# TensorE's MLP matmuls in program-text order instead of the scheduler's order

## The chip, the cores and the metric

The kernel runs on one core of a Trainium2 chip. The metric is the device time of one launch in microseconds (us): 2710.55 us, the median of three runs (2709.97 to 2710.85). Lower is better.

## The reference

One layer of a streaming encoder over 2048 prompt rows and 32 sample rows (2080 rows, width 1024). Phase 1 of the kernel computes the first five lines; the change concerns the sixth and seventh:

```
h  = RMSNorm(x);  p = h @ w_in                      # one combined projection
a  = pooling(p)      b = banded attention(p)
c  = gated DeltaNet(p)   d = GLA(p)
x  = x + concat(a, b, c, d) @ w_out
x2 = x
x  = x2 + square(relu(RMSNorm(x2) @ w_up)) @ w_down # hidden width 4096
y  = RMSNorm(x)
```

## The kernel before, in words

**Precision.** Each fp32 operand of a matmul is split in two: ScalarE (ACT) copies it to a rounded `hi` (L252), VectorE (DVE) subtracts to get `lo` (L253). A product is three matmuls: hi·hi, hi·lo, lo·hi.

**Tiling of the MLP** (`phase2`). Three blocks of rows: 696, 696 and 688 wide, each in two halves of h = 348, 348 or 344 columns. A block takes 16 steps f2 of 256 hidden units each:

- `mlp_up` (L1756) forms a step's hidden units with seven products of half-size operands instead of eight (a Strassen-Winograd scheme): (A11, B11), (A12, B21), (s2, T2), (s1, T1), (s3, T3), (s4, B22), (A22, T4). Each product is 12 matmuls of 128 x h, so a step has 84. They accumulate in three PSUM tiles (`ps` 1, 2 and 4 of a pool with one buffer each). ACT saves partial totals (L1779), DVE adds a saved one and a PSUM tile (L1782, `total`), squares (L1786) and splits the hidden units into the tile `u`.
- `mlp_down` (L1807) of the step before multiplies its two `u` tiles by w_down: 16 groups (two halves of 8) of 6 matmuls, 96 in all. Each group has its own PSUM tile `d` from a pool of **three** buffers (`pdn`); a DVE add (L1821) evicts it into the accumulators `acc`. In the last step of block 2 the two last downs are one, with 12 matmuls a group.
- The weights of a step are loaded by SP, `up_begin` (L1693) forms sums of w_up's quarters on GpSimd (POOL, L1699), and `up_weights` (L1706) splits them: five splits of 128x1024 and one of 128x512 a step on DVE.

**Beside the steps.** From f2 = 3 of blocks 0 and 1 on, for some four steps, the generator `mlp_keep` (L1644) normalises the next block's rows: squares on ACT (L1592), adds on DVE (L1594), sums (L1626 to L1638), stores to DRAM. In f2 = 15, `mlp_prep` (L1659) loads these back and splits them into `h2T` (14 pieces). After the last down of a block, `final` (L1842) normalises each half: `rstd` (L1566) sums squares over the partitions with three fp32 ones-matmuls (`g<-fs,c`), ACT takes Ln and Exp (L1572, L1573), and eight DVE multiplies (L1850) scale the rows, which are stored.

**What sets the order.** The program is written as a text of instructions; a scheduler reorders each engine's instructions by its own estimates and inserts the semaphores. Each engine then works strictly in its own order. In the text, the loop writes all of `mlp_up(f2)`, then all of `mlp_down` of f2 - 1, and the helper jobs' instructions where `tick` and `next(side)` call them. The scheduler's order for TensorE (PE) mixes up and down matmuls.

Of the kernel before, what the change touches and what calls it, by code (L numbers as in the profile page):

```python
# [110 lines left out]
class K:  # L111
# [1559 lines left out]
    def phase2(self):  # L1671
        nc, tc, a = self.nc, self.tc, self.a
        with ExitStack() as ctx:
# [168 lines left out]
            def final(acc, ts, t0, fs, end):  # L1842
                self.rstd(fs, ts.stop - ts.start)
                for i in range(8):
# [6 lines left out]
                    self.store(a["o_y"][i][:, t0 + ts.start:t0 + ts.stop], x, 2, eng=nc.scalar if end and i % 2 else nc.sync)  # L1851
                    yield 1

            for blk in range(3):
                _, n, h, _ = self.span(blk)
                chs = [slice(0, h), slice(h, n)]
                side = None
                us = []
                for f2 in range(17 if blk < 2 else 16):
                    if f2 == 15 and blk < 2:  # L1860
                        for _ in side:
                            pass
                        while not self.ready(("cb", blk + 1)):
                            self.tick()
                        side = self.mlp_prep(blk + 1, hT)
                    nxt = mlp_up(f2, h, side if f2 == 15 else None) if f2 < 16 else []
                    if blk < 2 and f2 == 3:
                        side = self.mlp_keep(blk + 1)
                    if f2 == 1 and blk:
                        self.drain(True)  # L1870
                        acc = []
                        for _ in self.mlp_acc(blk, acc):
                            pass
                    if f2 == 15 and blk == 2:

                        mlp_down(us + nxt, acc, chs, blk)
                    elif us:
                        mlp_down(us, acc, chs, blk, side)
                    us = nxt
                for _ in side or ():  # L1880
                    pass
# [80 lines left out]
```

## Time and profile before

| | |
|---|---|
| median time | 2710.55 us |
| profiled execution | 2718.81 us, of which the span is 2717.0 us |
| PE / DVE / ACT / POOL busy, share of the span | 96% / 72% / 40% / 32% |
| PE matmuls in the whole program | 17012 |
| chain that ended last | PE 48%, DVE 6%, DMA 4% |
| mean granted PE clock | 0.977 |

The profiled execution is 8.26 us above the median, all rows below are from it. "Busy" of PE counts matmuls; the weight loads (PEld) run beside them. In a timeline row the two first numbers are start and length in us, `x2` says that two instructions are joined in the row, and the bracket is the idle time of that engine before it and what ended it. The MLP runs from about 1277 us to the end.

### The profile page before, as it was taken

To read this page: it belongs to the slowest core of one execution; us is meant where nothing else is said; L and a number is where in the kernel's file an instruction comes from. 1 tells how busy PE (TensorE), PEld (TensorE's weight loads), DVE (VectorE), ACT (ScalarE), POOL (GpSimd) and SP (SyncE) were. 2 spreads that over 40 slices of the span, in tenths; PEclk is the share of its full clock that TensorE was granted. 3 is DMA by queue.
4 is the path that set the end of the run, shared out by engine and by line. 5 is a ranking of instruction groups with operands and counts; after the bars stand their busy time and mean duration, and the time that the engine had idled before them with its cause. 6 is when DMAs were issued, how large, how long until landed. Compare 5 with 4: busy or idle time off the path is not lost.

```text
span 2717.0 us, 44750 instructions
## 1 busy us (share of the span) xinstructions
PE 2598.6 (96%) x17012; PEld 2420.9 (89%) x17012; DVE 1958.6 (72%) x3498; ACT 1077.2 (40%) x1934; POOL 871.0 (32%) x1064
## 2 busy tenths in 40 slices
PE   7999998999899999998999999999999999999998
PEld 7887787788788877878999999988999999999998
DVE  6567778878886865566787667778767777766675
ACT  6435643653465343343433223442233343323232
POOL 4533564464446443322121112222212213221111
PEclk9998998999999989999999999999999999999999
DMA  5555454454545566366353222455222235222221
GB/s 166 172 152 161 125 177 147 130 156 139 152 136 164 156 174 197 110 203 210 105 179 114 70 70 80 137 173 174 94 70 86 73 109 162 78 63 86 71 72 48
DMA packets 229144, 349.21 MB, mean 129 GB/s; under 512 B 52032, under 2 KB 152784, under 8 KB 228928
## 3 DMA queue, kind: packets, MB, share of 16 engines
q1 hardware_dynamic: 162384, 295.49, 36.2%
q10 hardware_dynamic: 66480, 50.78, 5.7%
q8 instruction: 134, 2.20, 0.3%
q14 instruction: 82, 0.67, 0.1%
q0 software_dynamic: 64, 0.08, 0.0%
HBM read 273.83 MB, written 73.56 MB: 128 GB/s over the span
## 4 chain that ended last, share of the span: by engine, by line
PE 48%; DVE 6%; DMA 4%; issue 2%; ACT 1%; POOL 1%; SPq 0%; DVEq 0%; ACTq 0%; POOLq 0%
PE d L90 24%; PE u L90 19%; PE g L90 3%; DVE wx L253 1%; DVE acc L1821 1%; DVE wt L253 1%; DMA ldt<-w_o 1%; DVE h2T L253 1%; DMA x2d<-sg 1%; DVE acc L1850 1%; PE l L90 0%; DMA cb<-cbd 0%; POOL wur L1699 0%; DMA acc<-x2d 0%; DMA wur<-w_up 0%
## 5 line engine op out<-in xcount | busy, mean ns | idle before, releaser
L90 PE MATMUL d<-u,wt 128*128 128x348 f32 (+1 forms) x2400 | 631.1, 323 | 6.5 <-DVE acc L1821 5.6
L90 PE MATMUL d<-u,wx 128*128 128x348 f32 (+1 forms) x2208 | 601.8, 324 | 6.2 <-DVE acc L1821 6.1
L90 PE MATMUL g<-hT,wt 128*128 128x512 f32 (+2 forms) x2544 | 545.8, 363 | 16.4 <-DVE sg L1421 6.5
L1821 DVE TENSOR_TENSOR acc<-acc,d 128x348 f32<-128x348 f32 (+1 forms) x752 | 375.3, 510 | 210.5 <-PE d L90 203.0
L90 PE MATMUL u<-h2T,wt 128*128 128x348 f32 (+1 forms) x2024 | 515.0, 323 | 9.9 <-DVE wt L253 7.4
L90 PE MATMUL u<-h2T,wx 128*128 128x348 f32 (+1 forms) x2008 | 513.1, 323 | 1.3 <-ACT wt L252 0.8
L90 PEld LDWEIGHTS g<-hT,wt 128*128 128x128 f32 x2544 | 415.8, 195 | 79.5 <-DVE hT L256 5.6
L90 PEld LDWEIGHTS d<-u,wt 128*128 128x128 f32 x2400 | 428.0, 189 | 9.8 <-DVE acc L1821 7.4
L90 PEld LDWEIGHTS d<-u,wx 128*128 128x128 f32 x2208 | 397.3, 189 | 9.8 <-DVE acc L1821 9.2
L90 PEld LDWEIGHTS u<-h2T,wt 128*128 128x128 f32 x2024 | 357.3, 189 | 11.9 <-DVE wt L253 8.3
L90 PEld LDWEIGHTS u<-h2T,wx 128*128 128x128 f32 x2008 | 355.7, 189 | 2.7 <-ACT wt L252 1.0
L1699 POOL TENSOR_TENSOR s<-wur 128x512 f32<-128x512 f32 x48 | 72.4, 1508 | 642.3 <-DMA wur<-w_up 511.0
L90 PE MATMUL g<-wt,hT 128*128 128x256 f32 (+3 forms) x1632 | 246.6, 300 | 6.2 <-DVE sg L464 3.2
L90 PEld LDWEIGHTS g<-wt,hT 128*128 128x128 f32 (+1 forms) x1632 | 216.5, 191 | 16.1 <-DVE sg L464 3.9
L253 DVE TENSOR_TENSOR wt<-ldt,wt 128x1024 fp32r<-128x1024 f32 (+1 forms) x120 | 162.7, 1356 | 74.3 <-ACT wt L252 72.2
L252 ACT CAST wt<-wur 128x1024 fp32r<-128x1024 f32 x126 | 131.4, 1049 | 204.7 <-PE u L90 156.7
L1699 POOL TENSOR_TENSOR wur<-s,wur 128x512 f32<-128x512 f32 x48 | 65.3, 1361 | 418.6 <-DVE wt L253 220.4
L252 ACT CAST wx<-wur 128x1024 fp32r<-128x1024 f32 x114 | 118.8, 1048 | 202.8 <-PE u L90 164.2
L253 DVE TENSOR_TENSOR wx<-wur,wt 128x1024 fp32r<-128x1024 f32 x125 | 160.8, 1286 | 29.9 <-PE u L90 10.7
L252 ACT CAST wt<-ldt 128x1024 fp32r<-128x1024 f32 (+1 forms) x120 | 125.9, 1049 | 121.3 <-PE g L90 83.9
L253 DVE TENSOR_TENSOR wt<-wur,wx 128x1024 fp32r<-128x1024 f32 x114 | 146.5, 1288 | 31.9 <-PE u L90 14.7
L1779 ACT COPY k<-u 128x348 f32<-128x348 f32 (+1 forms) x144 | 64.1, 447 | 265.1 <-PE u L90 264.1
(348 smaller groups left out, 3819.8 us busy)
## 6 DMA issues: line engine op xcount, KB each, us to landing
wur<-w_up SPq DMA_DIRECT2D x96, 512.0 KB, 3.7
wur<-w_down SPq DMA_DIRECT2D x96, 512.0 KB, 3.7
ldt<-w_fm SPq DMA_DIRECT2D x56, 512.0 KB, 4.4
ldt<-w_o SPq DMA_DIRECT2D x32, 512.0 KB, 4.8
ldt<-w_tm SPq DMA_DIRECT2D x24, 512.0 KB, 4.0
fmd<-sg ACTq DMA_DIRECT2D x46, 256.0 KB, 2.9
qkr<-fmd SPq DMA_DIRECT2D x88, 128.0 KB, 3.6
tmd<-sg ACTq DMA_DIRECT2D x64, 128.0 KB, 2.8
```

Of the source, the lines that this page charges most:

```text
L90: return self.order(self.k.nc.tensor.matmul(out, lhsT, rhs, start=not have, stop=True, skip_group_check=True))
L252: nc.scalar.copy(hi, src)
L253: (eng or nc.vector).tensor_tensor(lo, src, hi.bitcast(F32), ALU.subtract)
L1699: add = lambda o, x, y: nc.gpsimd.tensor_tensor(o, x, y, ALU.add)
L1779: nc.scalar.copy(keep[n], ps[z].t[:, :h])
L1821: nc.vector.tensor_tensor(x, x, ps.t[:, :cw], ALU.add)
L1850: nc.vector.scalar_tensor_tensor(x, x, self.fg[:, i:i + 1], fs[0], ALU.mult, ALU.mult)
```

## The change

One line: before the loop over blocks, TensorE's instructions are put under a manual schedule, in which they stand in the order of the text. The other engines' orders still come from the scheduler, which now plans around PE's fixed order. No instruction is added or removed, on any engine.

```diff
+            ctx.enter_context(tc.manual_schedule(engines={mybir.EngineType.PE}))
             for blk in range(3):
                 _, n, h, _ = self.span(blk)
```

PE's order before, in the steady part of block 0: in step 8's up, `u_727`, `u_726`, `u_728` are its PSUM tiles, and `d_...` are groups of the down.

```order
L90 MATMUL u_726_15903<-h2T,wx 128x348
L90 MATMUL d_15762<-u,wx 128x348 x2
L90 MATMUL d_15762<-u,wt 128x348
L90 MATMUL d_15762<-u,wx 128x348 x2
L90 MATMUL d_15762<-u,wt 128x348
L90 MATMUL u_726_15903<-h2T,wx 128x348
L90 MATMUL u_726_15903<-h2T,wt 128x348
L90 MATMUL d_15770<-u,wx 128x348 x2
L90 MATMUL d_15770<-u,wt 128x348
L90 MATMUL d_15770<-u,wx 128x348 x2
L90 MATMUL d_15770<-u,wt 128x348
```

The same step's PE order now, at the end of its up and the first two groups of the down behind it (tile numbers differ by two):

```order
L90 MATMUL u_726_15905<-h2T,wt 128x348 x2
L90 MATMUL u_726_15905<-h2T,wx 128x348
L90 MATMUL d_16022<-u,wt 128x348 x2
L90 MATMUL d_16022<-u,wx 128x348
L90 MATMUL d_16022<-u,wt 128x348 x2
L90 MATMUL d_16022<-u,wx 128x348
L90 MATMUL d_16030<-u,wt 128x348 x2
L90 MATMUL d_16030<-u,wx 128x348
L90 MATMUL d_16030<-u,wt 128x348 x2
L90 MATMUL d_16030<-u,wx 128x348
```

Before, groups of a down stood between pieces of the next up; now 84 up matmuls are followed by 16 groups in one run.

DVE's order before, around the totals of the same up (`c<-k,u_...` is L1782, `acc<-acc,d_...` evicts a group):

```order
L1782 TENSOR_TENSOR c<-k,u_726_15903 128x348
L1821 TENSOR_TENSOR acc<-acc,d_15812 128x348
L1782 TENSOR_TENSOR c<-k,u_728_15905 128x348
L1786 SCALAR_TENSOR_TENSOR c<-c 128x696
L1821 TENSOR_TENSOR acc<-acc,d_15825 128x348
L253 TENSOR_TENSOR wx<-wur,wt 128x1024
L1821 TENSOR_TENSOR acc<-acc,d_15833 128x348
L1821 TENSOR_TENSOR acc<-acc,d_15842 128x348
L1786 SCALAR_TENSOR_TENSOR c<-c 128x696
L1821 TENSOR_TENSOR acc<-acc,d_15850 128x348
```

And now:

```order
L1782 TENSOR_TENSOR c<-k,u_728_15907 128x348
L1786 SCALAR_TENSOR_TENSOR c<-c 128x696
L253 TENSOR_TENSOR wt<-s_16170,wt 128x512
L253 TENSOR_TENSOR wt<-wur,wx 128x1024
L253 TENSOR_TENSOR u<-c,u 128x696
L1821 TENSOR_TENSOR acc<-acc,d_16022 128x348
L1786 SCALAR_TENSOR_TENSOR c<-c 128x696
L1821 TENSOR_TENSOR acc<-acc,d_16030 128x348
L1821 TENSOR_TENSOR acc<-acc,d_16039 128x348
L1821 TENSOR_TENSOR acc<-acc,d_16047 128x348
L253 TENSOR_TENSOR u<-c,u 128x696
```

The evictions, which were spread over the step, now stand in its second part; a square, two weight splits and a split of `u` stand ahead of the first of them.

DVE's order before at the end of block 0: `d_18480` is the eighth group of the last down, whose squares feed `rstd` of the first half.

```order
L1821 TENSOR_TENSOR acc<-acc,d_18480 128x348
L1836 TENSOR_TENSOR fs<-fs,sq 128x348
L1821 TENSOR_TENSOR acc<-acc,d_18497 128x348
L1821 TENSOR_TENSOR acc<-acc,d_18508 128x348
L1821 TENSOR_TENSOR acc<-acc,d_18520 128x348
L253 TENSOR_TENSOR wx<-wur,wt 128x1024
L1821 TENSOR_TENSOR acc<-acc,d_18533 128x348
L1821 TENSOR_TENSOR acc<-acc,d_18546 128x348
L1850 SCALAR_TENSOR_TENSOR acc<-acc,pv,fs 128x348 x8
L1821 TENSOR_TENSOR acc<-acc,d_18559 128x348
```

And now (`d_18482` is the eighth group):

```order
L1821 TENSOR_TENSOR acc<-acc,d_18482 128x348
L1836 TENSOR_TENSOR fs<-fs,sq 128x348
L1850 SCALAR_TENSOR_TENSOR acc<-acc,pv,fs 128x348 x8
L1821 TENSOR_TENSOR acc<-acc,d_18499 128x348
L1821 TENSOR_TENSOR acc<-acc,d_18510 128x348
L1821 TENSOR_TENSOR acc<-acc,d_18522 128x348
L1821 TENSOR_TENSOR acc<-acc,d_18535 128x348
```

The eight multiplies of `final` moved from behind the fifth eviction of the second half to ahead of the first. On PE the three matmuls of `rstd` moved with them: before, they stood behind the group `d_18533`, the fourth of the second half; now they stand directly behind `d_18482`:

```order
L90 MATMUL d_18482<-u,wt 128x348 x2
L90 MATMUL d_18482<-u,wx 128x348
L90 MATMUL g_18492<-fs,c 128x348 x2
L90 MATMUL g_18492<-sq,c 128x348
L90 MATMUL d_18499<-u,wt 128x348 x2
L90 MATMUL d_18499<-u,wx 128x348
```

Phase 1 and the out projection keep their order, but for two up matmuls ahead of the last out projection tile.

## Rows read from the trace of the kernel before

**Rows 1.** Busy time by stretch: us, busy by engine, granted PE clock, DMA.

```profile
1277.00:1440.00 163.00, 159.45 (x987) 156.02 (x986) 129.11 (x181) 62.40 (x89) 41.69 (x27) 1.00 0.48 150
1440.00:1700.00 260.00, 260.00 (x1636) 260.00 (x1634) 180.25 (x271) 79.92 (x111) 51.77 (x36) 1.00 0.26 77
1700.00:1910.00 210.00, 196.03 (x1162) 191.22 (x1162) 168.93 (x241) 78.99 (x120) 52.25 (x36) 0.97 0.51 158
1910.00:2190.00 280.00, 280.00 (x1757) 280.00 (x1756) 199.19 (x293) 91.55 (x126) 55.46 (x36) 1.00 0.29 88
2190.00:2300.00 110.00, 103.66 (x614) 100.99 (x613) 86.06 (x123) 43.19 (x67) 34.42 (x24) 0.95 0.42 130
2300.00:2670.00 370.00, 370.00 (x2350) 369.69 (x2349) 245.84 (x380) 109.84 (x152) 66.47 (x48) 1.00 0.23 70
2670.00:2717.00 47.00, 36.25 (x217) 34.00 (x215) 22.57 (x40) 13.74 (x26) 7.60 (x8) 0.92 0.17 61
```

**Rows 2.** PE's waits in the MLP: total us, times, longest.

```profile
PE d L90 <- DVE acc L1821: 11.6, 10, 2.5
PE u L90 <- DVE wt L253: 7.4, 3, 4.0
```

**Rows 3.** Chain of waits, steady part: start, length, what.

```profile
1503.01 2.87 PE d L90 x18
```

**Rows 4.** DVE's timeline in a steady step.

```profile
1569.66 0.88 DVE L1786 SCALAR_TENSOR_TENSOR c<-c 128x696 f32<-128x696 f32 x1
1570.47 1.22 DVE L253 TENSOR_TENSOR wt<-wur,wx 128x1024 fp32r<-128x1024 f32 x1
1571.60 0.51 DVE L1821 TENSOR_TENSOR acc<-acc,d 128x348 f32<-128x348 f32 x1
1572.51 0.52 DVE L1821 TENSOR_TENSOR acc<-acc,d 128x348 f32<-128x348 f32 x1 [0.40 <-PE d L90]
1572.95 0.92 DVE L253 TENSOR_TENSOR u<-c,u 128x696 fp32r<-128x696 f32 x1
1573.79 1.97 DVE L1786 SCALAR_TENSOR_TENSOR c<-c 128x696 f32<-128x696 f32 x1
...
1578.96 0.68 DVE L253 TENSOR_TENSOR wx<-s,wx 128x512 fp32r<-128x512 f32 x1
```

**Rows 5.** POOL's timeline in the same step.

```profile
1573.20 1.81 POOL L1699 TENSOR_TENSOR wur<-wur 128x512 f32<-128x512 f32 x1
```

**Rows 6.** DVE groups of the side jobs: count, busy us, mean ns, idle before.

```profile
L253 DVE TENSOR_TENSOR h2T<-cb,h2T 128x688 fp32r<-128x688 f32 x14 | 13.1, 945 | 2.3 <-ACT h2T L252 2.3
...
L1594 DVE TENSOR_TENSOR nss<-nss,xp 128x688 f32<-128x688 f32 x7 | 6.1, 871 | 4.6 <-ACT xp L1592 4.6
```

**Rows 7.** PE's timeline after a long and after a short wait.

```profile
1720.06 0.95 PE L90 MATMUL d<-u,wt 128*128 128x348 f32 x2 [2.25 <-DVE acc L1821]
...
1731.62 0.43 PE L90 MATMUL u<-h2T,wx 128*128 128x348 f32 x1 [0.50 <-DVE wx L253]
1731.89 0.48 PE L90 MATMUL u<-h2T,wt 128*128 128x348 f32 x2
```

**Rows 8.** PE's timeline: rstd in block 0, and at the kernel's end.

```profile
1768.43 1.33 PE L90 MATMUL g<-fs,c 128*128 128x348 f32 x4
...
2703.92 0.33 PE L90 MATMUL d<-u,wx 128*128 128x344 f32 x1
2705.74 1.42 PE L90 MATMUL g<-fs,c 128*128 128x344 f32 x4 [1.50 <-POOL fs L1836]
2707.00 0.74 PE L90 MATMUL g<-sq,c 128*128 128x344 f32 x2
```

**Rows 9.** DVE's timeline: the multiplies of final.

```profile
1772.37 5.78 DVE L1850 SCALAR_TENSOR_TENSOR acc<-acc,pv,fs 128x348 f32<-128x348 f32 x8 [0.52 <-ACT fs L1573]
...
2693.83 3.99 DVE L1850 SCALAR_TENSOR_TENSOR acc<-acc,pv,fs 128x344 f32<-128x344 f32 x8 [0.43 <-ACT fs L1573]
...
2708.88 4.42 DVE L1850 SCALAR_TENSOR_TENSOR acc<-acc,pv,fs 128x344 f32<-128x344 f32 x6 [4.09 <-ACT fs L1573]
```

## The prediction, made before the changed kernel ran

> **What bounds the kernel now.** I read the page's shares first: PE is busy 96% of the span, so the question is where the other 4% lies. The busy time by stretch answers that [rows 1]: from 1440 to 1700, 1910 to 2190 and 2300 to 2670 us PE is busy for all of 910 us. There is nothing to gain in them. PE's idle time in the MLP lies in four places: 163.00 - 159.45 = 3.6 us where the MLP begins, 210.00 - 196.03 = 14.0 around the end of block 0, 110.00 - 103.66 = 6.3 around the end of block 1, and 47.00 - 36.25 = 10.8 at the end. The last is nearly all the final norm after the last down matmul at 2703.92 [rows 8], which both orders have. So 23.9 us of idle time could go.
>
> Beside it lie slow matmuls. The granted clock's column gives 0.97 around the end of block 0 and 0.95 around that of block 1 [rows 1], so 0.03 x 210 + 0.05 x 110 = 11.8 us at most (part of it falls on idle time). PE's timeline shows what they are: after a wait of 2.25 us two matmuls take 0.95 us, after one of 0.50 us two take 0.48 [rows 7]. The first pair is at the lower level of 1.2 GHz, the second at 2.4 GHz. All that the old order loses ahead of the final norm is therefore 23.9 + 11.8 = 35.7 us. PE's list of waits says what it waits for: ten times an eviction (11.6 us) and three times a weight split (7.4 us) [rows 2], both DVE's work.
>
> At full speed 18 matmuls take 2.87 us in the chain of waits [rows 3], so one takes 0.1595. A product of 12 takes 1.91 us, an up of 84 13.4, a group of 6 0.96 and a down of 96 15.3; a step is 28.7 us.
>
> **The change part by part.** No instruction goes or comes. PE's 84 up matmuls are now one run, and its 16 groups another. This asks something new of DVE: the evictions all come within 15.3 us, one each 0.96 us, and three PSUM buffers let PE run three groups, 2.87 us, ahead. DVE has the capacity: in the clean stretches it is busy 180.25 of 260, 199.19 of 280 and 245.84 of 370 us [rows 1], 66 to 71%. The issue is what stands ahead of the evictions in its strict order.
>
> *Regular steps.* DVE instructions that follow each other without a wait start about 0.08 us before the end of the one ahead (1569.66 + 0.88 against 1570.47 [rows 4]); so a square costs 0.81, a 128x1024 split 1.13, the 128x512 split 0.60, a split of `u` 0.84 and an eviction or a total 0.43. An eviction starts about 0.36 us after its group's last matmul starts, which is also what I take for a total. The up's sixth product is done after 6 x 1.91 = 11.5 us, its total starts at 11.7. By the order now shown: square to 13.1, 128x512 split to 13.8, 128x1024 split to 14.95, split of `u` to 15.75, first eviction 15.66 to 16.2. PE has begun group 0 at 13.4 and wants a fourth buffer at 13.4 + 2.87 = 16.27: it waits some 0.06 us. The second square runs to 17.0, the second eviction to 17.4; PE wants its buffer at 17.23 and waits about 0.27. After that DVE needs 0.43 an eviction against PE's 0.96 and catches up. That is 0.33 us a step; 31 steps have this order of DVE: **10 us**.
>
> The bounds: nothing, if the square and the splits are a little earlier, and 1 us a step (31 us) if they are stretched. The stretch is in the trace: a square takes 0.88 us alone and 1.97 beside POOL's sum at 1573.20 [rows 4, 5]. POOL's next sums should start, by the time the raw weights land, about 19 us into the step, behind the two dangerous evictions; hence the low value.
>
> The Trainium skill ("SBUF — State Buffer", "Who interferes with whom") says that a DVE instruction with two inputs in SBUF excludes a GpSimd instruction that reads SBUF, for the whole instruction, and that one with a single SBUF input does not. The squares and splits are of the first kind and the 1.97 us agrees; an eviction, with one input in PSUM, is not, so by this rule only what stands ahead of evictions is stretched. It is the first rival below.
>
> *Weights.* In text order the splits for the next up have a whole down, 15.3 us, as lead, and `acc` loads of the next block a whole up more. The waits for weights [rows 2] and those around the block changes go. What remains is the start, where the first steps come as fast as before: **2 us** of the 3.6.
>
> *Side jobs in the first half of blocks 0 and 1.* `mlp_keep`'s adds on DVE wait for rows from DRAM through ACT, 4.6 us for seven in the old order [rows 6]. There, up matmuls were at hand for PE whenever an eviction was late; now an add that waits in DVE's queue holds the evictions behind it, and PE stops 2.87 us later. Reading the new DVE order with these durations I get 2.5, 0.5, 1.5 and 2.6 us for its four downs, so 7 a block: **14 us**, between 0 (rows early) and 20.
>
> *h2T.* In f2 = 15, DVE has 14 more splits of 0.945 us, 13.2 us [rows 6]. The rest of a step is 16 evictions (6.9), 5 large splits and a small one (6.3), 3 totals (1.3), 2 squares (1.6) and 2 splits (1.7), 17.8 us; together 31.0 against PE's 28.7. The old order spread the overload over neighbours, text order confines it: 2.3 us plus some order effects, **4 us** each, **8** for two; 3 to 8 each are the bounds.
>
> *The norm at the end of a block.* `rstd` now stands directly behind the eighth group. At the kernel's end this is what happens: the last down matmul starts at 2703.92 and the first of `rstd` at 2705.74 instead of 0.16 later [rows 8]: 1.66 us. In block 0 of the old order it ran among other matmuls with no wait (1768.43, [rows 8]). Its six passes to 2707.74 cost the same in both. The multiplies start 3.14 us after `rstd` begins (2708.88 - 2705.74 [rows 9]) and the eight take 3.99 to 5.78 [rows 9]; the next eviction is now behind them, at 3.14 + 3.99 + 0.45 = 7.6. PE has three buffers: 2.0 + 2.87 = 4.9. It waits 2.7, or 4.5 with the longer row; I take 3.0. With the second half's `rstd`, whose wait is the same 1.66, a block costs 1.66 x 2 + 3.0 = 6.3, two blocks **12.6 us**. The bounds are 0 (the wait for `fs` being covered by an early ACT) and 16.
>
> *Block 2's end.* The first half's `rstd` costs 1.7 again (its multiplies have groups of 12 matmuls as cover). The last up's `u` is wanted at once by the down that follows directly, behind 6 to 9 matmuls of cover; ACT's copy, square, ACT's `hi` and DVE's `lo` come to some 4 us, so 2.5. Together **4.2 us**.
>
> *Clock.* Each wait of more than 2 us is followed by some matmuls at the lower level, about 1 us lost as in [rows 7]; four such places give **4 us**.
>
> Sum: 10 + 2 + 14 + 8 + 12.6 + 4.2 + 4 = 54.8 us of losses now against 35.7 before: +19.1 us. On the profiled execution this is 2718.8 to 2737.9; the median lies 8.26 us below it, and I put the same difference on it: 2710.55 + 19.1 = 2729.7 us, rounded to **2730**.
>
> **Rivals.**
>
> *Every step loses (chance 0.14).* POOL's sums, or DVE's order, stretch the square and the split of `u` ahead of evictions, so that each of the 31 regular steps loses 1.0 to 1.6 us instead of 0.33: 31 x 0.7 to 31 x 1.3, 21 to 40 us more, 2751 to 2770. For it: the squares' 1.97 us. Against: POOL is busy only about 20% of the clean stretches (51.77 of 260) [rows 1].
>
> *Nothing net (0.14).* Side jobs and h2T cost half of what I think, the norm's wait is mostly hidden: 54.8 falls to 36, and the time stays within 0.2% of before. 0.2%, 5.4 us, is about what a measurement of this kernel can tell from no change; it is 2705.1 to 2716.0.
>
> *Text order is faster (0.14).* The mechanism is the lead of weights: before, PE's up ran ahead of its weights at the block changes (7.4 us [rows 2], with the slow matmuls behind); now no up can run ahead of the down before it, the weights always have 15 us. If the evictions keep up (DVE is under 71% busy), what is left is the norm (12.6), block 2's end (4.2) and the start (2): 18.8 against 35.7, 17 us less, 2694 us. It decides at side jobs and h2T together under 16 us with regular steps at zero. Against it: DVE's order, which puts four instructions ahead of the first eviction.
>
> *The clock falls in every step (0.03).* PE's short pauses between groups bring it to 1.2 GHz. With 1 us in 44 steps this would be 44 us more, about 2774. The pause of 0.50 us in [rows 7] is followed by full speed, so the row speaks against it. The Trainium skill ("TensorE: Matmul & The Clock Gate", "A second HAM failure mode: psum-queue depth-cycling") describes this, frequent small idle times between groups that cycle through PSUM; no row here shows it.
>
> *The change does nothing* is excluded: the orders differ in nearly every row of the MLP.
>
> **How the numbers follow.** The forecast, with its own range 2717 to 2745 from the terms' bounds taken partly, has 0.55; the rest are the rivals above. Slower by over 0.2%: 0.55 + 0.14 + 0.03 = 0.72; within: 0.14; faster: 0.14. The 8-in-10 range leaves out the far ends: 2700 to 2758.
>
> **What would show it.** In the profile after: the clean stretches have PE idle time of 0.3 us a step that ends with an eviction, just behind the first three groups of a down; PE's list of waits is led by evictions, some 30 us in all, and waits of `u` matmuls for weight splits are nearly gone; the `g<-fs,c` rows each have about 1.5 us of idle time ahead; behind them, the fourth group waits some 3 us for an eviction that follows eight L1850; the steps with h2T's splits and `mlp_keep`'s adds are longer than 28.7 us. The prediction is wrong if the regular steps show no wait and the side jobs' steps take 28.7 us (then faster), or if a regular step takes over 29.5 us (then much slower).

## The result: 2.3% slower, far beyond the forecast

The changed kernel takes 2772.12 us, the median of four runs (2767.12 to 2777.91), against 2710.70 in the same comparison: ratio 1.023, 95% interval 1.0211 to 1.0248. It is 61 us slower. The forecast was 2730 us, 2700 to 2758: the sign was right, the size was three times too small, and the time lies outside the range.

The two profiled executions differ by 48.3 us in span (2765.3 against 2717.0), less than the medians, because phase 1, which is the same in both, happened to be 14.7 us shorter in the one of after. The MLP itself is compared by PE's timeline: its first up matmul before, the same after, and the last down matmul after (before it starts at 2703.92 [rows 8]).

```profile
1277.16 0.80 PE L90 MATMUL u<-h2T,wt 128*128 128x348 f32 x4
```

```profile
1262.45 0.48 PE L90 MATMUL u<-h2T,wt 128*128 128x348 f32 x2
...
2753.42 0.32 PE L90 MATMUL d<-u,wx 128*128 128x344 f32 x1
```

That is 1426.8 us before and 1491.0 after: 64.2 us more, which is all of the difference of the medians. Both stretches hold the 24 matmuls of the out projection's last tile.

PE's waits in the MLP after (total, times, longest):

```profile
PE d L90 <- DVE acc L1821: 32.9, 25, 4.1
PE g L90 <- POOL fs L1836: 17.7, 6, 5.2
PE u L90 <- DVE c L1782: 3.8, 3, 2.7
```

Against [rows 2] the waits for weight splits are gone, as forecast; those for evictions have almost tripled, and those for the norm's sum, which had one wait of 1.5 us at the end, come to 17.7.

PE's busy time after, in the three stretches around which the old order lost time (columns as in [rows 1]):

```profile
1277.00:1440.00 163.00, 147.95 (x882) 143.92 (x881) 116.78 (x169) 56.06 (x79) 30.96 (x22) 0.97 0.39 120
1700.00:1910.00 210.00, 187.09 (x1093) 176.94 (x1092) 145.87 (x216) 79.52 (x118) 44.93 (x34) 0.97 0.40 125
2190.00:2300.00 110.00, 94.84 (x529) 87.89 (x528) 74.85 (x113) 42.07 (x65) 22.23 (x18) 0.94 0.39 126
```

PE is idle for 15.1, 22.9 and 15.2 us where it was 3.6, 14.0 and 6.3. The times are the same, the work in them not quite, since the MLP begins 14.7 us earlier here.

In the table the loss of a stretch of the MLP is its length between first matmuls in PE's timeline, less its matmuls at full speed: an up 13.4, a down 15.3 (13.2 and 15.1 in block 2), 1.49 us for each sum of the final norm, 0.90 for that of the next block's rows, 3.2 for the out projection's last tile. After the change the stretches end at 1297.68 (first two ups), 1446.53 and 1955.30 (rows), 1707.56, 2216.30 and 2718.28 (regular steps), 1807.21 and 2315.34 (block ends). The last column is an experiment that is told below.

| stretch | forecast | after | after, five PSUM buffers |
|---|---|---|---|
| first two ups | 2 | 5.3 | 7.0 |
| next block's rows, both | 14 | 35.1 | 8.7 |
| regular steps | 10 | 12.1 | about 0 |
| h2T, norm, next two ups, both block ends | 20.6 | 51.6 | 47.8 |
| last step | 4.2 | 3.7 | 5.0 |
| lower clock, not assigned | 4 | in the rows above | |
| sum | 54.8 | 107.8 | 68.5 |

The kernel before, by the same sum, lost 107.8 - 64.2 = 43.6 us.

The same 107.8 us can be parted by kind. In PE's timeline of the MLP, 60.5 us are idle time (23.6 before). Some 75 matmuls start 0.29 us apart without a wait, the lower level of 1.2 GHz, which is 10 us more than at full speed, and the norm's passes at that level cost 5 us more; before, 68 matmuls started so, 9 us. The rest is waits too short to show as idle and the first matmul behind each wait.

**Regular steps.** DVE's timeline of one, after:

```profile
1516.71 0.89 DVE L1786 SCALAR_TENSOR_TENSOR c<-c 128x696 f32<-128x696 f32 x1
1517.61 0.69 DVE L253 TENSOR_TENSOR wx<-s,wx 128x512 fp32r<-128x512 f32 x1
1518.22 1.22 DVE L253 TENSOR_TENSOR wx<-wur,wt 128x1024 fp32r<-128x1024 f32 x1
1519.36 0.88 DVE L253 TENSOR_TENSOR u<-c,u 128x696 fp32r<-128x696 f32 x1
1520.15 0.51 DVE L1821 TENSOR_TENSOR acc<-acc,d 128x348 f32<-128x348 f32 x1
1520.58 0.88 DVE L1786 SCALAR_TENSOR_TENSOR c<-c 128x696 f32<-128x696 f32 x1
1521.37 1.36 DVE L1821 TENSOR_TENSOR acc<-acc,d 128x348 f32<-128x348 f32 x3
```

This is the forecast's list, with its durations. No square is stretched by POOL: the longest of the 96 in the whole kernel takes 0.89 us, where the longest before took 2.00. PE's timeline gives the cost: one down starts at 1517.90, the next up at 1533.52.

```profile
1517.90 0.48 PE L90 MATMUL d<-u,wx 128*128 128x348 f32 x2
...
1533.52 0.48 PE L90 MATMUL u<-h2T,wx 128*128 128x348 f32 x2
```

The down takes 15.62 us for 96 matmuls that need 15.31, so it loses 0.31 us; the forecast was 0.33.

**The next block's rows.** The chain of waits after, to PE's stop of 3.62 us in the third down of block 0:

```profile
1339.45 2.86 DMA xp<-x2d
...
1347.25 4.12 DMA wur<-w_down
...
1355.47 1.29 POOL wur L1699
1356.78 1.05 ACT wt L252
1357.86 1.23 DVE wx L253
1359.09 0.28 DVE c L1782
...
1361.25 1.59 DVE c L1786 x2
1362.84 0.44 DVE acc L1821
...
1363.32 2.69 PE d L90 x8
```

Read it backwards: the eviction is behind two squares, these behind a total, and the total, whose PSUM tile PE had filled some 4 us before, stood in DVE's order behind a weight split (1357.86) that waited for ACT, for POOL's four sums, for raw weights, and these for a place among the four load buffers. In SP's queue all eight row loads stand ahead of them:

```profile
1323.55 18.59 SPq L1581 DMA_DIRECT2D xp<-x2d  x8
1344.12 1.89 SPq L1685 DMA_DIRECT2D wur<-w_up  x2
```

The first long stop of block 1 (3.07 us, 1873.34) has the same chain. The stops behind it have others: that of 2.17 us (1401.00) ends behind three instructions of `mlp_combine` and a split of `u`, and that of 4.08 (1430.19) goes back to a combination (L1638) for which DVE sat idle 3.27 us, because its buffer was still being stored. On PE's timeline:

```profile
1363.32 0.95 PE L90 MATMUL d<-u,wt 128*128 128x348 f32 x2 [3.62 <-DVE acc L1821]
1364.07 0.49 PE L90 MATMUL d<-u,wx 128*128 128x348 f32 x1
```

Behind this stop matmuls are at the lower level of 1.2 GHz, 0.29 us each, as in [rows 7]. The length of a stop alone does not tell whether that follows:

```profile
1401.00 0.59 PE L90 MATMUL d<-u,wx 128*128 128x348 f32 x2 [2.17 <-DVE acc L1821]
1401.43 0.32 PE L90 MATMUL d<-u,wt 128*128 128x348 f32 x1
...
1909.52 0.95 PE L90 MATMUL d<-u,wx 128*128 128x348 f32 x2 [1.09 <-DVE acc L1821]
1910.27 0.49 PE L90 MATMUL d<-u,wt 128*128 128x348 f32 x1
```

After 2.17 us the second matmul is at full speed already (the same after 2.69 us at 1295.67 and 3.07 at 1873.34); after 1.09 us, which follows a wait of 0.93, some ten are slow.

**The norm.** ACT's squares and POOL's sums of them at the end of block 0, then PE:

```profile
1750.22 0.49 ACT L1834 ACTIVATE sq<-acc 128x348 f32<-128x348 f32 x1 [1.04 <-POOL fs L1836]
1751.77 0.50 ACT L1834 ACTIVATE sq<-acc 128x348 f32<-128x348 f32 x1 [1.05 <-POOL fs L1836]
```

```profile
1750.79 0.94 POOL L1836 TENSOR_TENSOR fs<-fs,sq 128x348 f32<-128x348 f32 x1 [0.60 <-ACT sq L1834]
```

```profile
1755.97 2.69 PE L90 MATMUL g<-fs,c 128*128 128x348 f32 x4 [3.60 <-POOL fs L1836]
1765.12 0.58 PE L90 MATMUL d<-u,wt 128*128 128x348 f32 x2 [2.80 <-DVE acc L1821]
1776.21 2.69 PE L90 MATMUL g<-fs,c 128*128 128x348 f32 x4 [4.51 <-POOL fs L1836]
```

There is one buffer for squares; a square and its sum alternate each 1.5 us, while PE makes a group in 0.96. So `rstd` waits 3.6 us, not 1.5, and its passes run at the lower level: four take 2.69 us where they took 1.33 [rows 8]. The 2.80 us behind it is the wait behind the eight L1850 (forecast 3.0), as DVE's timeline shows:

```profile
1760.61 4.03 DVE L1850 SCALAR_TENSOR_TENSOR acc<-acc,pv,fs 128x348 f32<-128x348 f32 x8 [6.27 <-ACT fs L1573]
```

### The profile page after: what moved, and what is told of

It is laid out like the page before. It is cut to its first block, busy times and chain, and to the rows that moved or that the text cites. A ratio compares the mean times of both kernels' runs of the same rounds, so it can differ in the third digit from the quotient of the medians.

```text
span 2765.3 us, 44675 instructions
## 1 busy us (share of the span) xinstructions
PE 2612.0 (94%) x17012; PEld 2410.1 (87%) x17012; DVE 1931.9 (70%) x3498; ACT 1080.7 (39%) x1934; POOL 844.3 (31%) x1064
## 4 chain that ended last, share of the span: by engine, by line
PE 46%; DVE 5%; DMA 4%; issue 3%; POOL 3%; ACT 1%; SPq 0%; DVEq 0%; POOLq 0%; ACTq 0%
PE d L90 23%; PE u L90 17%; PE g L90 4%; POOL wur L1699 2%; DMA wur<-w_up 1%; DMA xp<-x2d 1%; DVE acc L1850 1%; DVE wx L253 1%; DVE wt L253 1%; PE l L90 0%; DVE acc L1821 0%; DMA ldt<-w_o 0%; DVE h2T L253 0%; DMA cbd<-cb 0%; POOL fs L1836 0%
## 5 line engine op out<-in xcount | busy, mean ns | idle before, releaser
L90 PE MATMUL d<-u,wt 128*128 128x348 f32 (+1 forms) x2400 | 643.2, 328 | 30.3 <-DVE acc L1821 28.5
L90 PE MATMUL g<-hT,wt 128*128 128x512 f32 (+2 forms) x2544 | 536.9, 359 | 16.3 <-DVE sg L1421 7.1
L90 PE MATMUL u<-h2T,wt 128*128 128x348 f32 (+1 forms) x2024 | 502.8, 321 | 4.3 <-DVE c L1782 3.8
L90 PE MATMUL u<-h2T,wx 128*128 128x348 f32 (+1 forms) x2008 | 498.9, 321 | 4.3 <-ACT c L1803 2.4
L90 PEld LDWEIGHTS g<-hT,wt 128*128 128x128 f32 x2544 | 408.6, 191 | 77.8 <-DVE hT L256 5.6
L253 DVE TENSOR_TENSOR wx<-wur,wt 128x1024 fp32r<-128x1024 f32 x125 | 153.5, 1229 | 90.9 <-ACT wt L252 66.6
```

Of the source, the lines that this page charges most:

```text
L90: return self.order(self.k.nc.tensor.matmul(out, lhsT, rhs, start=not have, stop=True, skip_group_check=True))
L253: (eng or nc.vector).tensor_tensor(lo, src, hi.bitcast(F32), ALU.subtract)
```

## The experiments

All ratios are against the kernel before, with their 95% intervals; the changed kernel's is 1.023.

**Which steps make the loss.** The first pair put the manual schedule around each call (`text` is true for f2 = 7 to 14, in block 2 for 2 to 14, or for the others):

```diff
-                    nxt = mlp_up(f2, h, side if f2 == 15 else None) if f2 < 16 else []
+                    with guard(text):
+                        nxt = mlp_up(f2, h, side if f2 == 15 else None) if f2 < 16 else []
...
+                    with guard(text):
                         ...
                             mlp_down(us, acc, chs, blk, side)
```

> Text order only in the regular steps (up and down of f2 = 7 to 14 in blocks 0 and 1, 2 to 14 in block 2: 29 of 48 steps), the scheduler's order in the others. Theory A (the loss is made where DVE also serves side jobs: the next block's rows, h2T, the norm; a regular step loses 0.31 us as the steady part of the trace after shows): 29 x 0.31 = 9 us plus 0 to 4 us where one order goes over into the other, 2719 to 2724 us. Theory B (text order costs in every step, and the profile's steady part shows only a lucky execution): 61 x 29/48 = 37 us, about 2748 us.

Measured 0.9999 (0.9986 to 1.0012).

> The complement: text order only in the other 19 steps (start, the next block's rows, h2T, the norm, the last step), the scheduler's order in the 29 regular ones. Theory A: all of the loss but some 10 us, 2757 to 2766 us. Theory B: 61 x 19/48 = 24 us, about 2735 us.

Measured 1.0008 (0.9993 to 1.0024). Neither theory had this: the parts add up to 2 us of 61. The orders explain it: a manual schedule around one call fixes the order within that call alone, and the scheduler still put the groups of a down between the pieces of the next up. So the edit was not the one that the expectations spoke of; what it shows is that text order *inside* an up or a down costs nothing. By exclusion the loss comes from not mixing the two.

The second pair holds one manual schedule over a whole stretch:

```diff
+                    if text != was:
+                        held.close()
+                        if text:
+                            held.enter_context(tc.manual_schedule(engines={mybir.EngineType.PE}))
+                        was = text
```

> As the first experiment, but text order held over each whole stretch of regular steps (f2 = 7 to 14 of blocks 0 and 1, 2 to 14 of block 2), so that no group of a down can slip between pieces of the next up. Theory A (a regular step in text order costs 0.31 us, the rest of the loss is made where DVE serves side jobs): some 28 x 0.31 = 9 us over the kernel before, with 1 to 4 us for the crossings 0.2 to 0.5% slower. Theory B (each step costs its share of the 61 us): 36 us, 1.3% slower.

Measured 0.9987 (0.9974 to 0.9999), so no loss. PE's downs in the stretch take 15.6 us in blocks 0 and 1, a loss of 0.3 us each as forecast, but the stretches left to the scheduler lost less than before: PE's idle time from the first up to the last down is 14.5 us against 23.6 before.

> The complement: text order held over the other stretches (f2 = 15 of a block to f2 = 6 of the next, and the last step). Theory A: 61 - 9 = some 50 us, 1.7 to 2.0% slower than before. Theory B: 25 us, 0.9%.

Measured 1.0215 (1.0186 to 1.0244): 58 of the 61 us. That is a little over theory A's 1.7 to 2.0%. Theory B is out; theory A holds for the place of the loss.

**The jobs for the next block.** The calls of `mlp_keep` and `mlp_prep` are taken out:

```diff
-                    if f2 == 15 and blk < 2:
-                        ...
-                        side = self.mlp_prep(blk + 1, hT)
-                    if blk < 2 and f2 == 3:
-                        side = self.mlp_keep(blk + 1)
```

> The changed kernel without the work for the next block's rows: mlp_keep and mlp_prep are left out, blocks 1 and 2 multiply block 0's h2T. Theory A (the rows' DVE instructions, which wait for loads, stores and ACT, stand ahead of evictions: 34 us; the 14 splits in one step: 17 us): 42 to 52 us less than the changed kernel, about 0.2 to 0.7% slower than the kernel before. Rival G (PE stops in text order at the block changes for other reasons, such as late weights): under 25 us less.

Measured 1.0064 (1.0040 to 1.0088): 45 us less than the changed kernel (1.66% of the kernel before), within theory A's 42 to 52; in PE's timeline the MLP is 47 us shorter. Its waits:

```profile
PE g L90 <- POOL fs L1836: 17.7, 6, 5.3
PE d L90 <- DVE acc L1821: 7.1, 6, 2.8
```

The waits for evictions fall from 32.9 to 7.1 us, the norm's stay at 17.7: the norm's part of the loss does not come from these jobs.

**How far PE may run ahead.**

```diff
-                        ps = PT(self, pdn, [P, 512], "d")
+                        nd[0] += 1
+                        ps = PT(self, self.pg, [P, 512], "g") if nd[0] % 5 > 2 else PT(self, pdn, [P, 512], "d")
```

> The changed kernel, with the PSUM tiles of a down's groups taken from five buffers instead of three (two of every five from the pool that phase 1 used), so that PE can be five groups (4.8 us) ahead of DVE's evictions instead of three (2.87 us). Theory A (PE stops because evictions stand behind other work in DVE's order for 3 to 7 us at a time): the regular step's 0.31 us goes (12 us), each wait for an eviction shrinks by up to 1.9 us and with it part of the slow matmuls behind it; 25 to 38 us less, 2734 to 2747 us; the waits for the norm's sum stay. Rival C (DVE has too much work in those steps, so that a longer queue only moves the wait): under 8 us less, 2763 or more.

Measured 1.0099 (1.0076 to 1.0122): 1.31% or 36 us less than the changed kernel, at the upper end of theory A. The table has where: the regular step's loss is gone and the rows' is a quarter, but the block ends keep 47.8 of their 51.6 us. Its waits (the wide `g` tiles are downs too):

```profile
PE g L90 <- POOL fs L1838: 26.0, 6, 7.2
PE g L90 <- DVE acc L1823: 4.7, 7, 1.1
...
PE d L90 <- DVE acc L1823: 2.1, 4, 1.0
```

Evictions: 6.8 us instead of 32.9. The norm: 26.0 instead of 17.7. Counted from the first matmul of the last up of block 0, PE arrives at the norm 4.4 us earlier than in the changed kernel, while the sum is done only 2.5 us earlier.

**The norm.**

```diff
             def final(acc, ts, t0, fs, end):
+                if not end:
+                    yield 6 if ts.start else 3
                 self.rstd(fs, ts.stop - ts.start)
```

> The changed kernel, with the norm's sum over partitions (rstd) written three groups later for the first half of a block and six products later for the second half (not for the last half of all). Theory A (31 us in all of the two block ends: two waits of 3.6 to 5.2 us for fs each, the slow matmuls behind them, and an eviction behind the eight multiplies): both waits for fs nearly go, the one for the eviction stays; 16 to 24 us less, 2748 to 2756 us. Rival D (the wait is for the chain of squares, and what is held back is wanted just as late elsewhere): under 6 us less, 2766 or more.

Measured 1.0204 (1.0178 to 1.0230), 0.26% or 7 us less, a difference that lies within the two intervals. In PE's timeline each block end is 10 us shorter (99.7 to 89.5 us for the one of block 0) and the MLP 16.6. Three rows show the steps:

```profile
1764.48 1.44 PE L90 MATMUL g<-fs,c 128*128 128x348 f32 x4 [0.78 <-POOL fs L1836]
1772.48 0.95 PE L90 MATMUL d<-u,wt 128*128 128x348 f32 x2 [2.17 <-DVE acc L1821]
...
1786.54 1.33 PE L90 MATMUL g<-fs,c 128*128 128x348 f32 x4
```

The waits for `fs` went as theory A says, the one for the eviction stayed. The trace supports the size that theory A names, the times alone do not.

```diff
-                                    (nc.vector if i % 2 and (blk == 2 or i > 4) else nc.gpsimd).tensor_tensor(...)
+                                    (nc.vector if blk < 2 or i % 2 else nc.gpsimd).tensor_tensor(...)
```

> The changed kernel with the sums of squares of the last norm (fs, L1836) in blocks 0 and 1 all on DVE instead of five of seven on POOL. In the trace after, a square and its POOL add follow each other every 1.5 us because there is one buffer for squares, while PE makes a group each 0.96 us. Theory E (that pace makes rstd wait 3.6 and 4.5 us in text order): with DVE's 0.5 us add a pair takes 1.1 us, the waits for fs fall to 1 to 2 us and with them the slow matmuls behind; 8 to 16 us less than the changed kernel, 0.3 to 0.6%. Rival F (the waits come from evictions that are late behind DVE's other work): with more work on DVE no gain or a loss.

Measured 1.0250 (1.0220 to 1.0279): no gain. The trace has E's mechanism: ACT's squares follow each other in 1.08 us, and the four waits for `fs` are 2.25, 3.69, 2.24 and 4.17 us instead of 3.60, 4.51, 3.56 and 5.24. The second halves gain least, since the last sum now stands in DVE's queue behind a weight split of 1.22 us and itself takes 1.5 us instead of 0.5. In PE's timeline the two block ends are 4.1 and 3.7 us shorter; but with DVE's order planned anew some 7 us came back elsewhere, most of it in the first two ups and the rows of block 1. So the pace explains about 1.35 of the 3.60 us of a first half; 2.25 stay, of which 1.5 is what the kernel's end has too. As a cure the edit failed.

**What in the rows' job stops PE.**

```diff
-                        if side is not None and i % 2:
+                        if side is not None and (i % 2 if done or us[0][0] == 28 else i % 4 == 3):
```

> The changed kernel with the job for the next block's rows (mlp_keep) called once in four groups of a down instead of once in two, so that it lasts some eight steps instead of four. In the trace after, the long waits of PE in these downs (3.6, 2.2 and 4.1 us) come when DVE's queue is headed by an instruction that waits: a weight split whose raw weights were loaded late, a combination whose buffer is still being stored. Theory H (it is the density: loads, stores and DVE's work of a row crowd into 1.9 us): at half the rate most of the 34 us goes, 15 to 28 us less than the changed kernel, 0.6 to 1.0%. Rival I (each such wait stops PE whenever it comes): the same number of waits over more steps, under 6 us less.

Measured 1.0205 (1.0182 to 1.0228): 7 us less, by the times nearer to rival I, and a difference that lies within the two intervals. The longest wait for an eviction falls from 4.1 to 2.4 us and the total from 32.9 to 22.9, but there are 29 of them instead of 25. In PE's timeline the MLP is 15.7 us shorter, the lower end of theory H. As with the norm the two measures differ, so H and I are not told apart.

```diff
-        x = self.ld.tile([P, 4 * 280], F32, name="xp", tag="ld")
+        x = self.cb.tile([P, 696], F32, name="xp", tag="cb") if acc is None else self.ld.tile([P, 4 * 280], F32, name="xp", tag="ld")
```

> The changed kernel, with the next block's rows (xp, L1581) loaded into the three buffers that mlp_combine uses later (cb), no longer into the four of the raw weights (ld); the scheduler then places these loads and the norm's squares earlier. In the chain of waits of the changed kernel the stop of 3.6 us at 1359.7 goes back over evictions, totals behind a weight split, POOL's sums and a late weight load to five row loads in the same buffers. Theory J (rows in the weights' buffers make the weights late, and a split that waits heads DVE's queue): the losses of the first two downs with rows go in each block, 10 to 18 us less than the changed kernel, 0.4 to 0.7%. Rival K (what counts is DVE's own work for the rows in these downs, wherever the loads land): under 4 us less.

Measured 1.0240 (1.0200 to 1.0280): no gain. In PE's timeline the waits in the second and third down of block 0, 0.21 and 3.62 us, are gone: these downs lose 0.4 and 0.3 us instead of 1.7 and 5.3, and the same two of block 1 lose 0.3 each instead of 1.6 and 3.3. With 0.6 us in the down ahead of block 1's that makes 11 us, as J says of the place. The downs behind them, with the combinations, lose about what they lost. But the scheduler put the rows of block 2 at the end of block 0 (loads at 1736.7 to 1753.1 us), which became 7.6 us longer, and there PE's first wait for the norm grew:

```profile
1762.05 2.69 PE L90 MATMUL g<-fs,c 128*128 128x348 f32 x4 [6.28 <-POOL fs L1836]
```

The stop moved with the work. J is right on its places, some 11 of the rows' 35 us, and wrong on the sum; how the other 24 part between DVE's own work and the waits for stores stays open.

**Versions that beat both.**

> The kernel before, in the scheduler's order throughout, with five PSUM buffers for the groups of a down. Its list of waits had 11.6 us for evictions, with slow matmuls behind: if five buffers cover them, 5 to 14 us less than before (0.2 to 0.5%). If the waits at its block changes are DVE's backlog and not buffers: no change.

The edit for five buffers in the kernel before: 0.9929 (0.9911 to 0.9946), 2686.81 us. That is 19 us less, more than the 5 to 14 expected. PE's waits for evictions fall from 11.6 to 5.6 us.

> Text order over the regular stretches, the scheduler's order elsewhere, and five PSUM buffers. The regular step's 0.31 us goes (28 x 0.31 = 9 us), and some of the 11.3 us for which PE still waits for evictions; against the run with three buffers (0.9987 of before) 8 to 18 us less: 0.4 to 0.8% faster than the kernel before. If the order of the block changes gets worse with it, no better than that run.

Five buffers with text order in the regular stretches: 0.9916 (0.9894 to 0.9937), 2686.24 us, the fastest; its interval overlaps with that of the run above, so text order adds nothing that is shown.

> Text order everywhere, with what the experiments point to together: five PSUM buffers, rstd held back, sums of squares on DVE, the next block's rows at half the rate. Each was argued to take away a part of the 103 us that the changed kernel loses: steady 12, rows some 25 of 34, norm some 25 of 31, h2T some 9 of 17. That leaves 30 to 40 us, about what the kernel before loses (39): 0.3% faster to 0.3% slower than before. If text order has a cost that these do not touch, 0.6% slower or more.

Measured 0.9965 (0.9945 to 0.9985): a little beyond the better end of what was expected. Text order everywhere is then 0.35% faster than the scheduler's with three buffers: together the edits take back the whole 61 us and some more. Against the scheduler's order with five buffers alone (0.9929) it is 0.36%, 10 us, slower: a cost of text order that these edits do not reach is not ruled out.

> The same edit in the fastest kernel so far (text order in the regular stretches, five PSUM buffers, 0.9916 of before). There PE has other matmuls and five groups of lead at these places, so its list of waits has little of this kind: 0 to 4 us less by theory J; no change by K.

Measured 0.9955 (0.9932 to 0.9978), no better than without the edit (0.9916): J's 0 to 4 us did not show. In PE's timeline the MLP is 0.7 us longer, which is K's "no change"; with so few waits left this says little between the two.

## Why the prediction was wrong

**Right.** PE's and DVE's orders do what was read from them. The regular step: 0.31 us for 0.33, and the rival "every step loses" was rightly held unlikely, as was the clock falling in every step (granted 1.00 from 1446 to 1707 us, with 0.3 us lost in each). Weight waits are gone. The last step: 3.7 for 4.2. The wait behind the eight L1850: 2.8 and 1.7 for 3.0.

**Wrong: the next block's rows, 14 against 35.1 us.** The step "Reading the new DVE order with these durations I get 2.5, 0.5, 1.5 and 2.6 us for its four downs, so 7 a block" took DVE's durations and a wait for the rows themselves. In block 0 these downs lost 1.7, 5.3, 2.9 and 8.1 us. It did not follow who else waits for the row loads: SP's queue had the rows ahead of the step's raw weights in the same four buffers, and a weight split that waits stands ahead of totals, squares and evictions. Nor did it follow a combination that waits for the store of its buffer. The long stops were 3.6, 2.2 and 4.1 us in block 0. Even the upper bound of 20 us was too low. Without these jobs and h2T 45 us go; with five groups of lead, three quarters of the rows' loss goes. The chain of waits is shown for the single stops named above, not for the whole 35 us.

**Wrong: the norm's wait, 1.66 us each against 3.6 to 5.2.** The row was taken from the kernel's end [rows 8], where a group has 12 matmuls and lasts 1.9 us: there a square and its sum, 1.5 us, keep up with PE. In blocks 0 and 1 a group lasts 0.96 us. The row was near in kind but came from a place with another pace. With a faster pace the first half's wait is 2.25; held back by three groups, it falls to 0.8.

**Too small: the clock, 4 us for four places.** The forecast let each wait of more than 2 us be followed by about 1 us at the lower level. There were eleven waits of 2 us or more, the slow matmuls came behind some of them and behind some shorter ones, and the norm's passes ran at the lower level too (2.69 for 1.33 us, four times): 15 us in all.

**Too small: h2T and the start.** h2T came to some 7.8 us a block against 4: 5.8 in the down, where evictions stand behind the splits, and 2.0 in the up, in two short waits for ACT's copies and for totals. The first two ups lost 5.3 us against 2, most of it in a wait of 2.69 us for a total and one of 1.32 for ACT.

**Too small on the other side: the old order's loss, 35.7 against 43.6.** Idle time and the clock column left out waits too short to show as idle and the first matmul behind each wait. It made the forecast 8 us too slow and so, by luck, hid a part of the error: the new losses were short by 53 us.

The range failed because two terms left their own bounds: the rows' 35.1 us stood under at most 20, and the norm's, 51.6 less h2T's 15.7, under at most 16. All upper bounds together, 31 + 2 + 20 + 16 + 16 + 4.2 + 4 = 93.2 us, would have given 2768 us, still below the 2772.12 measured. What regular steps, rows and h2T share is the lead: in text order a lateness of DVE beyond 2.87 us reaches PE. Five buffers, 4.8 us, test that sentence: the regular step's loss goes, the rows' falls to a quarter and h2T's to about 4 us a block, but the norm's waits grow from 17.7 to 26.0 us, so it does not hold for them.

## What to carry to other kernels

When an order takes away what an engine could do instead, price each waiting instruction by everything behind it in its queue, and by the lead that the buffers between the engines give: here three PSUM buffers against five were worth 36 us in text order and 19 in the scheduler's. Before a duration is carried from one place to another, compare the pace of the engines that feed it at both. And test the order over the stretch it is meant for: fixed inside single calls it cost nothing.

## What the runs showed that was not expected

Fixing PE's order in one stretch changed the scheduler's plan in others for the better: text order in the regular steps cost some 9 us there (0.3 us a step), and PE's idle time fell by 9. Loss removed from one place came back elsewhere in two experiments, in which DVE's order was planned anew with the edit. Whether matmuls ran at the lower level behind a stop did not follow from its length: not after 3.07 us, but after 1.09. And phase 1, the same instructions in the same order, varied between profiled executions by up to 17 us (first up matmul at 1260 to 1277 us), so that two spans alone would have understated this change by a quarter.
